# When the scan of one head pair may begin: waits taken per half instead of per pair, in a planned hybrid RWKV-7/GLA layer

## The chip, the cores and the metric

The kernel runs on one core of a Trainium2 chip. The metric is the device time of one execution in microseconds (us); lower is better. The engines that matter are TensorE (PE in the profile, PEld for its weight loads), VectorE (DVE), ScalarE (ACT), GpSimd (POOL) and SyncE (SP), which issues DMAs.

## The reference, cut to what matters

One layer over 256 latent tokens and 256 context tokens, width 2048, all in float32. A combined projection feeds an RWKV-7 branch (16 heads of 64 channels) and a GLA branch (4 heads); both scan in two directions, context first. The change lies in the RWKV-7 branch, whose recurrence for one head and one direction is

```
sa = S a_t
S  = S * w_t + sa b_t^T + v_t k_t^T
y  = S r_t
```

After it, the summed output `wkv` of both directions is normalized per head and token (mean and variance over 64 channels), gets a bonus term, is gated and goes through `w_a`; the GLA branch goes through `w_b`; the gated sum of both goes through `w_out`, the residual and a final RMSNorm.

## The kernel before, in words

Every float32 weight matrix is split into a high and a low part, and each product is three matmuls (`wH`, `wL` with the high and low part of the activations). This is the dense work; it comes as jobs of one 128-column slice each, in a list, and `stream` feeds them to TensorE. The RWKV-7 branch is done by eight head pairs `p`; a pair holds two heads in the 128 partitions.

The order of all instructions is made by a planner (`Issue`) when the program is built. Each piece of work is a generator (a track) that yields either an operation or list of operations, a claim on a PSUM bank, or a condition on a set `DONE`. `Issue.run` keeps an estimated clock for each engine and always emits the operation that can start earliest by these estimates; among PE operations within a small distance it takes the track with the lowest priority number, and the dense stream has 99, so that it fills what the others leave. The engines then run their queues in the emitted order, and hardware semaphores carry the real dependences. A condition on `DONE` is thus no instruction: it decides from which point in the emitted order on a track's operations may be placed. `Op` has the costs that the planner reckons with; for a two-input operation on POOL it is

```
149 + (1.667 if any(q == 0 and k > 1 for x in ins for q, k in x.ap[1:]) else 2.096) * n
```

nanoseconds for n elements per partition.

Tracks of a pair `p`: `fe_track` (features: decays, rates, keys; its second part asks for `gg`, `bt` and `bv` of pair p-1), `v_track` (loads values), `ab_track` and `inv_track` (a triangular inverse by 30 steps of two POOL operations each, `tm<-M` and `M<-M,tm`, a DVE transpose `Lin<-M`, PE products `pH` and `pZ`, and the evacuation into `Z`; it ends with `("gi", p)`), `gg_track` (chunk products into `GM` and `GMr`, six evacuations in three twos: context chunks, latent chunks 4 and 5, latent chunks 6 and 7), `bt_track` (transposed update rows into `BK`, for each direction `d` two groups `g` of four chunks), `mv_track` (transposed values into `UV`, two groups of four chunks; the group g asks that the scan of pair p-1 has passed step 4g+3), `aq_track` (copies by DMA), and `sc_track`, the scan.

`sc_track` makes eight steps: steps 0 to 3 over the context chunks and 4 to 7 over the latent ones, both directions at once. A step is a chain through four PE products and their evacuations: `p<-UV,GM`, `R<-p`, `pU<-R,Z`, `UV<-pU`, `pSs<-UV,BK`, `Sn<-pSs` and `UV<-Sn`. After step 7 it emits `("sc1", p)`, then waits for `("post", p-1)`, takes the mean of the output (`mu<-pY`, `xc<-pY,mu`), emits `("sc", p)`, and goes on with the normalization, the transpose `pyt`, the bias `yt` and the gate, and ends with `("post", p)`. `bv_track` of pair p+2 waits for `("post", p)`.

When the last pair's features and products are out, `"C"` is in `DONE`, and the jobs of the two branch projections may be taken once the jobs before them are done: first the 32 gate jobs (`tg`), then 16 slices of `w_b`, then 16 of `w_a`, whose activations are `yH` and `yL`, one slice per pair. The second half of each `w_a` slice asks for the normalized output of pair 7.

Of the kernel before, what the change touches and what calls it, by code (L numbers as in the profile page):

```python
# [76 lines left out]
class Issue:  # L77
# [136 lines left out]
    def rel(self, x):  # L214
        nm = x.tensor.name
        b = self.bank_of.pop(nm)
        self.busy.discard(b)
        self.bank_free[b] = self.rd.get(nm, 0.0)
# [112 lines left out]
def hybrid_layer(tc, a, out):  # L331
    nc = tc.nc
    es = ExitStack()
    with es:
# [331 lines left out]
        DONE = set()  # L666
# [423 lines left out]
        def past(p, i):  # L1090
            return lambda: p < 2 or ("st", p - 2, i) in DONE

        def bt_track(p, d, bk):

            BK = RW["BK"][p % 2]
            for g in range(2):
                yield past(p, 4 * g + 3)
                pt = yield Claim("g3", [P, 4, P], "pbt", bk)
                yield [PE.transpose(pt[:, n, :], bk[:, 4 * g + n].rearrange("p a b -> p (a b)"), ident) for n in range(4)]
                o = BK[:, :, 4 * g:4 * g + 4, d, :].rearrange("p h i c -> p i h c")  # L1100
                yield AC.copy(o if d == 0 else o[:, ::-1], pt.rearrange("p n (h c) -> p n h c", h=2))
                rel(pt)
            DONE.add(("bt", p) if ("bt", p, 1 - d) in DONE else ("bt", p, d))

        def ab_track(p, xp):

# [12 lines left out]
        def gg_track(p, fp, xp):  # L1119

            yield lambda: ("ab", p) in DONE
            s = RW[p]
            ar, bks = s["ar"], s["bks"]
            GM, GMr, BK = s["GM"], s["GMr"], s["BK"] = tuple(RW[n][p % 2] for n in ("GM", "GMr", "BK"))
            vs = rows(p)[1]
            xk = 1 - p % 2
            left = [6]

            def done():
                left[0] -= 1  # L1130
                if not left[0]:
                    DONE.add(("gg", p))

            def mask(m, n, r):
                return m[r, p % 2, None].to_broadcast([r.stop - r.start, n, 2, 64])

            def ev_c(pg, hd):
                yield DV.tensor_tensor(GM[vs, hd, 0:4], pg[vs], mask(m_ab, 4, vs), op=OP.mult)
                rel(pg)
                done()  # L1140

            def ev_l(pg, hd, i):
                yield DV.tensor_tensor(GM[vs, hd, 4 + i:6 + i], pg[vs, :, :, 0, :], mask(m_ab, 2, vs), op=OP.mult)
                yield DV.tensor_tensor(GMr[:, hd, i:i + 2], pg[:, :, :, 1, :], mask(m_r, 2, slice(0, P)), op=OP.mult)
                rel(pg)
                done()

            yield past(p, 3)
            pg = []
            for hd in range(2):  # L1150
                pg.append((yield Claim("g3", [P, 4, 2, 64], f"pgc{hd}", *bks, ar)))
            yield [PE.matmul(pg[hd][vs, i, d, :], bks[d][half(hd), chunk(i, d), xk, :], ar[half(hd), d, i, 0, :],
                             start=True, stop=True) for i in range(4) for d in range(2) for hd in range(2)]
            for hd in range(2):
                iss.spawn(3, ev_c(pg[hd], hd), "evc")
            iss.spawn(3, aq_track(p, xp), "aq")
            for i in (0, 2):
                yield past(p, 5 + i)
                pg = []
                for hd in range(2):  # L1160
                    pg.append((yield Claim("g3", [P, 2, 2, 2, 64], f"pgl{hd}", *bks, ar)))
                yield [PE.matmul(pg[hd][:, ii, d], bks[d][half(hd), chunk(4 + i + ii, d)].rearrange("p a b -> p (a b)"),
                                 ar[half(hd), d, i + ii, 1:3, :], start=True, stop=True)
                       for ii in range(2) for d in range(2) for hd in range(2)]
                for hd in range(2):
                    iss.spawn(3, ev_l(pg[hd], hd, i), "evl")
# [71 lines left out]
        def mv_track(p, fp, xp):  # L1238

            yield lambda: ("vc", p) in DONE  # L1240
            UV, vc = RW["UV"], RW["vc", p]
            vs = rows(p)[1]
            for g in range(2):
                yield lambda: p == 0 or ("st", p - 1, 4 * g + 3) in DONE
                pV = yield Claim("g3", [P, 2, 2, 64], "pV", vc)
                yield [PE.transpose(pV[:, x].rearrange("p h v -> p (h v)"), vc[:, 256 * g + P * x:256 * g + P * x + P], ident)
                       for x in range(2)]
                for par in range(2):
                    i0, i1 = 4 * g + par, 4 * g + 3 - par
                    yield AC.copy(UV[vs, i0:i0 + 3:2, 0], pV[half(par)])  # L1250
                    yield AC.copy(UV[vs, i1 - 2:i1 + 1:2, 1], pV[half(par), ::-1])
                rel(pV)
            DONE.add(("vdone", p))
            DONE.add(("mv", p))

        def sc_track(p, xp):

            yield lambda: all((x, p) in DONE for x in ("gi", "aq", "mv", "bt")) and (p == 0 or ("sc", p - 1) in DONE)
            s = RW[p]
            Dt, GM, GMr, BK, Z = (s[x] for x in ("Dt", "GM", "GMr", "BK", "Z"))  # L1260
            UV, rq = RW["UV"], RW["rq"]
# [1 line left out]
            DH = [(d, hd) for d in range(2) for hd in range(2)]  # L1263
            pY = Sc = None
            for i in range(8):
                if i == 4:
                    pY = yield Claim("py", [P, 4, 64], "pY")
                    yield PE.matmul(pY.rearrange("p c v -> p (c v)"), zb[:, 0:P], zb, start=True, stop=False,
                                    skip_group_check=True)
                p1 = yield Claim("st", [P, 2, 64], "p1", *(UV[:, i, :, hd, :] for hd in range(2)))  # L1270
                kr = slice(0, P) if i else vs
                b = [PE.matmul(p1[half(hd), d, :], GM[kr, hd, i, d, :], UV[kr, i, d, hd, :], start=True, stop=True)
                     for d, hd in DH]
                if i > 0:
                    SD = xp.tile([P, 2, 64], F32, name="SD", tag="SD", bufs=1)
                    b += [AC.activation(SD[:, d, :], Sc[:, d, :], AF.Copy, scale=Dt[:, i, d:d + 1]) for d in range(2)]
                yield b
                if i >= 4:
                    yield [PE.matmul(pY[half(hd), chunk(i, d) - 4, :], rq[us, d, i - 4, hd, :], UV[us, i, d, hd, :],
                                     start=False, stop=False, skip_group_check=True) for d, hd in DH]  # L1280
                R = xp.tile([P, 2, 64], F32, name="R", tag="R", bufs=1)
                yield AC.copy(R, p1)
                rel(p1)
                pU = [None, None]
                for hd in range(2):
                    pU[hd] = yield Claim(("st", "u1")[hd], [P, 2, 64], f"pU{hd}", R)
                yield [PE.matmul(pU[hd][half(hd), d, :], Z[half(hd), 2 * i + d, :], R[half(hd), d, :], start=True, stop=True)
                       for d, hd in DH]
                yield [(DV.tensor_copy if hd else AC.copy)(UV[us, i, :, hd, :], pU[hd][half(hd)]) for hd in range(2)]
                rel(pU[0])  # L1290
                rel(pU[1])
                pS = yield Claim("st", [P, 2, 64], "pSs", *(UV[:, i, :, hd, :] for hd in range(2)))
                yield [PE.matmul(pS[half(hd), d, :], BK[:, hd, i, d, :], UV[:, i, d, hd, :], start=True, stop=True)
                       for d, hd in DH]
                if i >= 4:
                    yield [PE.matmul(pY[half(hd), chunk(i, d) - 4, :], GMr[:, hd, i - 4, d, :], UV[:, i, d, hd, :],
                                     start=False, stop=i == 7, skip_group_check=True) for d, hd in DH]
                Sn = xp.tile([P, 2, 64], F32, name="Sn", tag="Sn", bufs=2)
                if i == 0:
                    yield [DV.tensor_scalar(Sn[:, d, :], pS[:, d, :], Dt[:, i, d:d + 1], None, op0=OP.mult) for d in range(2)]  # L1300
                else:
                    yield [DV.scalar_tensor_tensor(Sn[:, d, :], pS[:, d, :], Dt[:, i, d:d + 1], SD[:, d, :],
                                                   op0=OP.mult, op1=OP.add) for d in range(2)]
                rel(pS)
                Sc = Sn
                DONE.add(("st", p, i))
                if i < 7:
                    yield [(AC.copy if hd else DV.tensor_copy)(UV[us, i + 1, :, hd, :], Sn[half(hd)]) for hd in range(2)]
# [503 lines left out]
```

## Time and profile before

| | before |
|---|---|
| median of 3 runs | 1364.46 us (1361.43 to 1368.26) |
| the profiled execution's own time | 1361.36 us |
| its span, first to last instruction | 1359.6 us |
| mean granted TensorE clock | 0.977 of full speed |
| PE busy | 1270.1 us (93%) |
| DVE, ACT, POOL busy | 968.3, 718.2, 543.3 us |

The span is what the trace covers; the execution's own time holds 1.76 us more around it. Almost every instruction is recorded on line 304, since a helper emits them, so groups are told apart by the tiles they write and read (`UV<-pV` is written UV, read pV). The eight scans lie between about 690 and 1158 us.

### The profile page before, as it was taken

The numbers are of one execution on the slowest core, as the hardware profiler recorded it, in microseconds if no ns is written. First come the engines' busy times: TensorE is split into PE (matmuls) and PEld (weight loads), VectorE is DVE, ScalarE is ACT, GpSimd is POOL, SyncE is SP. The second block draws the span as 40 slices with busy tenths as digits, with TensorE's granted clock in tenths as the row PEclk, the third lists the DMA queues.
The fourth block names the chain that finished last, engine by engine and source line by source line (L and its number), as shares of the span: only waits on it lengthen the run. The fifth ranks groups of instructions, "written<-read, shape, count | busy, mean of one in ns | idle before, by whom it ended". The sixth has DMA issues, their size and how long they took to land. (4 is left out here: it accounts for less than half of the span.)

```text
span 1359.6 us, 29662 instructions
## 1 busy us (share of the span) xinstructions
PE 1270.1 (93%) x11479; PEld 1068.1 (79%) x11479; DVE 968.3 (71%) x2031; ACT 718.2 (53%) x1449; POOL 543.3 (40%) x684
## 2 busy tenths in 40 slices
PE   5999999999999999999899999799989999999996
PEld 3555578688788897998777778677878888999876
DVE  4433497885965737767978998698978776668656
ACT  5222244343334444486577678667766666445443
POOL 0000476676570000005888729673983550000012
PEclk9999999999999999999889999799979999999999
DMA  9999465455462433576632443234433545789564
GB/s 347 354 340 311 132 195 168 150 171 160 145 202 79 134 102 97 153 196 171 157 85 76 113 118 92 77 99 114 108 78 94 138 105 145 203 247 271 185 230 144
DMA packets 311186, 220.45 MB, mean 162 GB/s; under 512 B 37354, under 2 KB 286724, under 8 KB 310532
## 3 DMA queue, kind: packets, MB, share of 16 engines
q1 hardware_dynamic: 311044, 218.55, 55.5%
q8 instruction: 90, 1.47, 0.4%
q14 instruction: 52, 0.43, 0.1%
HBM read 199.76 MB, written 12.46 MB: 156 GB/s over the span
## 5 line engine op out<-in xcount | busy, mean ns | idle before, releaser
L304 DVE TENSOR_TENSOR wL<-raw,wH 128x512 fp32r<-128x512 f32 x484 | 377.2, 786 | 170.2 <-ACT wH L304 165.0
L304 ACT CAST wH<-raw 128x512 fp32r<-128x512 f32 x484 | 295.1, 616 | 328.5 <-PE acc L304 208.7
L304 PE MATMUL acc<-lH,wH 128*128 128x256 f32 x896 | 285.1, 318 | 0.5 <-ACT tg L304 0.5
L304 PE MATMUL acc<-lL,wH 128*128 128x256 f32 x896 | 256.0, 286 | 0.0
L304 PE MATMUL acc<-lH,wL 128*128 128x256 f32 x896 | 255.6, 285 | 0.2 <-DVE wL L304 0.2
L304 PEld LDWEIGHTS acc<-lH,wH 128*128 128x128 f32 x896 | 173.4, 194 | 21.1 <-issue 4.5
L304 POOL TENSOR_TENSOR tm<-M 64x30 f32<-64x30 f32 (+14 forms) x240 | 160.1, 667 | 74.3 <-DVE M L304 48.1
L304 POOL TENSOR_TENSOR M<-M,tm 64x30 f32<-64x30 f32 (+14 forms) x240 | 170.1, 709 | 18.7
L304 PEld LDWEIGHTS acc<-lL,wH 128*128 128x128 f32 x896 | 174.5, 195 | 3.1 <-issue 1.7
L304 PEld LDWEIGHTS acc<-lH,wL 128*128 128x128 f32 x896 | 173.9, 194 | 0.4 <-DVE wL L304 0.4
L304 PE MATMUL acc<-hH,wH 128*128 128x512 f32 (+1 forms) x416 | 168.7, 406 | 1.3 <-ACT lo L304 1.3
L304 PE MATMUL acc<-hH,wL 128*128 128x512 f32 (+1 forms) x416 | 157.2, 378 | 0.0
L304 PE MATMUL acc<-hL,wH 128*128 128x512 f32 (+1 forms) x416 | 156.3, 376 | 0.1
L304 PEld LDWEIGHTS acc<-hH,wH 128*128 128x128 f32 x416 | 78.6, 189 | 38.1 <-issue 22.9
L304 POOL TENSOR_TENSOR xs<-yg,fg 128x512 f32<-128x512 f32 (+1 forms) x10 | 13.5, 1371 | 231.4 <-DVE yg L304 231.4
L304 POOL TENSOR_TENSOR gw<-gw,csl 128x512 f32<-128x512 f32 x60 | 71.1, 1185 | 61.9 <-DMA gw<-in_w_mod_dram 61.9
L304 PEld LDWEIGHTS acc<-hH,wL 128*128 128x128 f32 x416 | 78.4, 188 | 15.5 <-DVE wL L304 0.4
L304 POOL TENSOR_TENSOR ga<-ga,gw 128x512 f32<-128x512 f32 x60 | 88.6, 1476 | 4.2
L304 PEld LDWEIGHTS acc<-hL,wH 128*128 128x128 f32 x416 | 78.9, 190 | 10.6 <-DVE hL L304 0.4
L304 PE MATMUL acc<-yH,wH 128*128 128x256 f32 x256 | 73.0, 285 | 0.0
L304 PE MATMUL acc<-yL,wH 128*128 128x256 f32 x256 | 72.8, 284 | 0.0
L304 PE MATMUL acc<-yH,wL 128*128 128x256 f32 x256 | 72.8, 284 | 0.0
(318 smaller groups left out, 2627.7 us busy)
## 6 DMA issues: line engine op xcount, KB each, us to landing
raw<-in_w_in_dram SPq DMA_DIRECT2D x174, 512.0 KB, 4.0
wm<-in_w_mod_dram SPq DMA_DIRECT2D x64, 512.0 KB, 6.9
gw<-in_w_mod_dram SPq DMA_DIRECT2D x64, 256.0 KB, 4.0
raw<-in_w_out_dram SPq DMA_DIRECT2D x32, 512.0 KB, 4.8
raw<-in_w_b_dram SPq DMA_DIRECT2D x16, 512.0 KB, 4.1
raw<-in_w_a_dram SPq DMA_DIRECT2D x16, 512.0 KB, 4.9
kv<-kvo SPq DMA_DIRECT2D x16, 256.0 KB, 3.9
tg<-tg SPq DMA_DIRECT2D x32, 128.0 KB, 3.8
```

The costliest lines, as they stand in the source:

```text
L304: op = Op("dma" if name == "dma_start" else self.key, name, lambda: f(*a, **k), aps[0], aps[1:], func, k.get("accum_out"), any(x.tensor.na ...
```

## The change

`sc_track` of pair p started when `gi`, `aq`, `mv` and `bt` of its pair were all complete and `("sc", p-1)` was there, that is, after the subtraction of the mean of pair p-1. It now starts at `gi`, `aq`, `("sc1", p-1)` (step 7 of pair p-1 emitted) and group 0 of the values, of both directions' update rows and of the chunk products. Group 1 of values and update rows and the next two evacuations of chunk products are asked for before step 4, the last two before step 6. No operation is added, removed or changed.

```
-            DONE.add(("bt", p) if ("bt", p, 1 - d) in DONE else ("bt", p, d))
+                DONE.add(("bt", p, d, g))
+            if ("bt", p, 1 - d, 1) in DONE:
+                DONE.add(("bt", p))
...
             def done():
                 left[0] -= 1
+                if left[0] % 2 == 0:
+                    DONE.add(("gg", p, 6 - left[0]))
                 if not left[0]:
                     DONE.add(("gg", p))
...
                 rel(pV)
+                DONE.add(("mv", p, g))
             DONE.add(("vdone", p))
-            DONE.add(("mv", p))
 
         def sc_track(p, xp):
 
-            yield lambda: all((x, p) in DONE for x in ("gi", "aq", "mv", "bt")) and (p == 0 or ("sc", p - 1) in DONE)
+            def there(g):
+                return lambda: all(x in DONE for x in (("mv", p, g), ("bt", p, 0, g), ("bt", p, 1, g), ("gg", p, 2 + 2 * g)))
+
+            yield lambda: ("gi", p) in DONE and ("aq", p) in DONE and (p == 0 or ("sc1", p - 1) in DONE)
+            yield there(0)
...
             for i in range(8):
+                if i == 6:
+                    yield lambda: ("gg", p, 6) in DONE
                 if i == 4:
+                    yield there(1)
```

## Rows read from the trace of the kernel before

**Rows 1.** The page's busy times: engine, busy us (share) x instructions.
```profile
PE 1270.1 (93%) x11479; PEld 1068.1 (79%) x11479; DVE 968.3 (71%) x2031; ACT 718.2 (53%) x1449; POOL 543.3 (40%) x684
```

**Rows 2.** Windows: stretch, length, busy per engine (instructions), granted clock, DMA share, GB/s.
```profile
690.00:1121.00 431.00, 397.42 (x5127) 338.62 (x5126) 359.83 (x782) 300.83 (x654) 292.91 (x430) 0.95 0.39 100
1121.00:1158.00 37.00, 36.86 (x435) 31.44 (x434) 21.54 (x57) 22.24 (x64) 0.00 (x0) 1.00 0.52 140
1158.00:1257.00 99.00, 99.00 (x835) 98.76 (x836) 73.38 (x154) 48.22 (x89) 0.00 (x0) 1.00 0.84 245
```

**Rows 3.** The chain that ended last: start, us, what.
```profile
1172.27 84.60 PE acc L304 x705
```

**Rows 4.** Tiles tg and yH: duration ns min/median/max, first and last start.
```profile
L304 ACT ACTIVATE tg<-acc x32: 362/380/397, 589.1 to 1164.4; 128x256 f32<-128x256 f32 x32
...
L304 PE MATMUL acc<-yH,wH x256: 279/283/387, 1163.7 to 1256.3; 128*128 128x256 f32 x128
...
L304 ACT CAST yH<-yt x1: 400/400/400, 1169.4 to 1169.4; 128x256 fp32r<-128x256 f32 x1
```

**Rows 5.** Timeline, scan of pair 0 to scan of pair 1: start, us, instruction.
```profile
747.71 0.48 DVE L304 SCALAR_TENSOR_TENSOR Sn<-pSs,Dt,SD 128x64 f32<-128x64 f32 x2
...
749.49 0.42 DVE L304 TENSOR_TENSOR xc<-pY,mu 128x256 f32<-128x256 f32 x1
...
750.82 0.36 ACT L304 COPY UV<-pV 64x256 f32<-64x256 f32 x1
...
751.41 0.31 PEld L304 LDWEIGHTS p<-UV,GM 64*64 64x64 f32 x8
```

**Rows 6.** Windows: last Sn of a pair to first R of the next, seven times.
```profile
748.20:751.90 3.70, 3.70 (x43) 3.24 (x41) 3.46 (x10) 2.65 (x7) 3.31 (x6) 1.00 0.87 193
797.40:801.10 3.70, 3.70 (x77) 3.37 (x76) 3.58 (x12) 3.53 (x9) 0.00 (x0) 1.00 0.83 212
860.20:882.00 21.80, 20.00 (x244) 17.26 (x242) 14.85 (x34) 19.14 (x29) 12.39 (x22) 0.79 0.27 70
936.40:951.10 14.70, 11.74 (x105) 9.94 (x102) 10.87 (x30) 12.57 (x21) 9.98 (x20) 0.88 0.34 87
1009.60:1012.50 2.90, 2.90 (x35) 2.44 (x34) 2.31 (x7) 1.92 (x6) 2.59 (x5) 1.00 0.14 17
1067.80:1071.80 4.00, 4.00 (x46) 3.54 (x43) 3.30 (x12) 3.65 (x10) 3.45 (x8) 1.00 0.92 198
1113.20:1121.20 8.00, 8.00 (x146) 7.39 (x142) 6.99 (x20) 6.88 (x14) 0.00 (x0) 1.00 0.38 101
```

**Rows 7.** Timeline, scan of pair 3 to scan of pair 4.
```profile
940.00 0.41 DVE L304 TENSOR_TENSOR xc<-pY,mu 128x256 f32<-128x256 f32 x1
...
941.33 1.12 PE L304 MATMUL pbt<-ident,bk 128*128 128x128 f32 x4 [2.96 <-ACT BK L304]
...
948.66 1.28 ACT L304 COPY UV<-pV 64x256 f32<-64x256 f32 x4
```

**Rows 8.** Timeline, the last evacuation into Z of pairs 3, 5 and 7.
```profile
874.98 0.69 DVE L304 COPY Z<-pZ 32x512 f32<-32x512 f32 x1
...
1008.36 0.69 DVE L304 COPY Z<-pZ 32x512 f32<-32x512 f32 x1 [0.58 <-ACT Z L304]
...
1120.30 0.69 DVE L304 COPY Z<-pZ 32x512 f32<-32x512 f32 x1 [0.20 <-ACT Z L304]
```

**Rows 9.** Timeline, the longest PE stall among the scans.
```profile
857.68 2.03 DVE L304 STREAM_TRANSPOSE Lin<-M 64x1024 f32<-64x1024 f32 x1 [5.61 <-POOL M L304]
...
859.76 1.06 PE L304 MATMUL pH<-Lin,GMo 32*32 32x32 f32 x32 [6.89 <-DVE Lin L304]
```

**Rows 10.** Window: the stretch of that stall and what followed it.
```profile
852.50:866.00 13.50, 6.61 (x98) 6.12 (x92) 6.98 (x13) 4.72 (x6) 6.34 (x16) 0.62 0.09 29
```

**Rows 11.** Timeline, one POOL operation of the inverse in two of the eight pairs.
```profile
842.72 2.66 POOL L304 TENSOR_TENSOR M<-M,tm 64x220 f32<-64x220 f32 x1
...
1094.31 1.11 POOL L304 TENSOR_TENSOR M<-M,tm 64x220 f32<-64x220 f32 x1
```

## The prediction, made before the changed kernel was run

> **What bounds the kernel now.** I read the page's busy times first: PE is busy 93% of the span, the next engine 71% [rows 1]. A share over the whole span says little here, so the windows come next: among the scans (690 to 1121 us) PE is busy 397 of 431 us, in the last scan nearly always, and from 1158 to 1257 us without a gap [rows 2]. The chain that ended last says the same of that stretch: one piece of 84.6 us made of dense matmuls alone [rows 3]. So the question is what a scan's end releases. Pair 7's normalized output becomes `yH` at 1169.4 us [rows 4]. Its readers are the second halves of the `w_a` slices. The branch matmuls on `yH` run from 1163.7 to 1256.3 us, and the 16 slices of `w_b` are the first half of them, so the `w_a` half begins near 1163.7 + 92.6/2 = 1210 us. The last scan is some 40 us early. What waits behind the scans is not their result but PE's own backlog: the last of the 32 gate jobs is evacuated at 1164.4 us [rows 4], after the last scan step, so there was dense work to be had during all eight scans.
>
> From this follows the rule by which I cost the change. PE has a fixed amount of work. If a scan begins earlier, the dense matmuls that filled its wait are done later, at the same price, in the stretch where PE never stops. The end moves only by PE time that was idle, or that ran at half clock.
>
> **The handovers.** The change acts between the last `Sn` of one pair and the first `R` of the next. I looked at the timeline of one of them: `Sn` of pair 0 is written by 748.19 us, the mean is subtracted by 749.91, the second group of pair 1's values is copied by 751.18, and the first products of scan 1 load their weights at 751.41 [rows 5]. The last to come was thus the value copy, not the normalization: the group may be transposed only after step 7 of the pair before, and the old condition wanted it for step 0. The windows of the seven handovers sum to 58.8 us [rows 6]. Two of them the change can't shorten: `Z` of pair 3 is complete at 875.67 and of pair 7 at 1120.99 us [rows 8], near the ends of these waits, and `("gi", p)` is still asked for. The other five are 3.7, 3.7, 14.7, 2.9 and 4.0, together 29.0 us.
>
> **What is removed.** From the old start to `R` the products and the copy take about 1 us (751.41 to the window's end at 751.9, and as much for the hand-over of `Sn`: an estimate). The five waits could shrink by 29.0 - 5 x 1.0 = 24.0 us, of which pair 4 has 13.7. For pair 5 this holds only while its scan stays behind `Z`, which is ready at 1009.05 us, 0.5 us before the handover [rows 6, 8]; once the scan of pair 4 ends 13.7 us earlier, scan 5 waits for its inverse instead. So the scan chain gains between 24 us, if the inverses move up with it, and 3.7 + 3.7 - 2.0 = 5.4 us up to pair 3, where `Z` was last in any case.
>
> What is that worth on PE? In the five waits PE is busy 3.70 + 3.70 + 11.74 + 2.90 + 4.00 = 26.04 of 29.0 us [rows 6]. The idle rest, 2.96 us, is one wait, of `pbt` for a copy on ACT [rows 7]. The granted clock in that window is 0.88 of full; at the half level (1.2 instead of 2.4 GHz) this is 0.12/0.5 = 24% of 14.7, 3.5 us, worth half of it, 1.7 us. Bounds: nothing, if the `pbt` wait stays where it is, and 2.96 + 1.7 = 4.7 us, if the earlier scan fills it. I take 4.7, since with scan 4 under way PE has something else in its queue just there.
>
> **What is moved.** The instructions are the same, DMAs included. The mean and its subtraction (0.41, 0.17 and 0.42 us in the handover) now lie beside the first step of the next scan on DVE, 1.0 us per pair, covered by the 40 us that the last scan is early; without that cover 7 us. PSUM bank of `pY`: it is claimed at step 4, over 20 us later, so nobody waits.
>
> **What is added.** New conditions: second group of values and update rows before step 4, products before steps 4 and 6. A scan takes about 50 us for eight steps (751.9 to 797.4 us, 882.0 to 936.4 [rows 6]), so step 4 is some 20 us after step 0, while the copies of the second value group end 3 us after the scan before in pair 1 and 14 in pair 4 [rows 5, 7]. I cost them at nothing; if the cover were gone, step 4 of one pair would wait up to the 14 us, again beside dense work.
>
> **The sum.** 1361.36 us (the profiled execution) - 4.7 = 1356.7. The median of the runs shown is 3.1 us above the profiled execution, so on that scale 1359.8; I say 1360. On this kernel about 0.5%, 6.8 us, is what a measurement can tell from no change.
>
> **Rivals.** The emitted order of everything after the first handover will differ, and the engines run their queues in that order. This gives a rival on each side.
>
> *B, faster: the stalls go.* Among the scans PE is idle 431 - 397.4 = 33.6 us, and a granted clock of 0.95 costs up to 0.05 x 431 = 21.6 us more [rows 2]. The largest piece is at 852.9: 6.89 us in which `pH` waits for a DVE transpose, which waits 5.61 us for POOL [rows 9], and then a stretch at clock 0.62 of 13.5 us, worth 0.38 x 13.5 = 5.1 us if PE were busy in it [rows 10]. If the new order puts this transpose further back, 6.9 + 5.1 = 12.0 us go besides the 4.7: 1361.4 - 16.7 + 3.1 = 1348. For it: a stage that is up to 24 us shorter has less time for stalls. Against it: the stall comes from POOL, which the change does not touch.
>
> *C, slower: the inverse comes too late for the new order.* The planner's cost for the POOL operation with 220 elements is 149 + 2.096 x 220 = 610 ns; it took 1.11 us in one pair and 2.66 in another [rows 11]. So the planner believes an inverse done earlier than it is, and puts the transpose and `pH` into the queues of DVE and PE where they may have to wait, with everything behind them. The old waits of 24 us gave POOL time to catch up, with dense work in them; a tighter order takes that time out and returns it as stalls that nothing fills. It decides where a transpose stands in DVE's queue ahead of POOL's last step. Price: one more stall as the one shown, 12.0 us, at pair 5, where the advance by then could be 19 us, and one of 5.4 us at pair 3: 1361.4 + 17.4 + 3.1 = 1382; with one alone 1370 to 1377. The Trainium skill speaks for this rival: SBUF — State Buffer, section "Who interferes with whom", says that a DVE instruction with both inputs in SBUF and a GpSimd instruction exclude each other on a shared port, so that the later one waits for the whole of the other. The trace agrees so far as the same POOL operation varies from 1.11 to 2.66 us [rows 11]; by this rule DVE work packed closer would make inverses longer still, and C would lie at its upper price; by the row alone either price could come.
>
> *D: the starts don't move,* since `gi` or the inverse's chain is last everywhere: 1361.4 + 3.1 = 1364.5. Against it: five handovers in which `Z` was ready before the values.
>
> The same skill's TensorE: Matmul & The Clock Gate, section "What's actually happening", says that the clock is low unless activity keeps it up. The trace agrees: the window around the idle 6.89 us has a granted clock of 0.62 [rows 10]. It makes each stall of B and C dearer than its idle time, which their prices already hold from the row.
>
> **How the numbers follow.** Forecast 0.44 (0.30 within 0.5%, 0.12 faster, 0.02 slower), B 0.28 (0.26 faster, 0.02 the same), C 0.23 (0.22 slower, 0.01 the same), D 0.05 (0.03 the same, 0.02 slower). Faster 0.38, the same 0.36, slower 0.26. The forecast's own range is 1354 to 1367: 1359.8 with the 4.7 us missed, or with half of B's 12.0 us added. The range for 8 in 10 reaches to B with a second stall of the 4.7 us kind gone (1348 - 4.7 = 1343) and to C (1382, with little beyond 1380): 1342 to 1380.
>
> **What would show it.** Right: the first `R` of pairs 1, 2, 4 and 6 within about 1 us of the last `Sn` before; the scans' end earlier by 5 to 24 us; more dense matmuls after it, at the same rate; PE's idle time among the scans smaller by 3 us and not much else. B: the 6.89 us wait of `pH` gone, the clock in the windows higher. C: more or longer waits of `Lin<-M` for POOL and of `pH` for DVE, and PE busy less of the stretch. The prediction is wrong if PE's idle time in the stage moves by more than 7 us either way, or if PE runs out of dense work.

## The result, and the profile after

The changed kernel took 1372.43 us (median of 8 runs, 1366.45 to 1377.9) against 1364.09 us for the kernel before (8 runs, 1359.0 to 1370.16). The ratio is 1.0061, 95% interval 1.0032 to 1.0090: slower by a little more than the half per cent that I had set as the bound. I had forecast 1360 us.

The page of the changed kernel begins with its busy times, as [rows 1]:

```profile
span 1372.0 us, 29669 instructions
...
PE 1273.9 (93%) x11479; PEld 1068.6 (78%) x11479; DVE 965.8 (70%) x2031; ACT 717.3 (52%) x1449; POOL 547.8 (40%) x684
```

The number of matmuls is the same. The span is 12.4 us longer; 3.8 us of that is time in which PE is busy and 8.6 us time in which it is idle. The medians differ by only 8.3 us: each profile shows one execution, the one before a fast one of its kernel, the one after a slower one of its own. So some 4 us of what this pair of profiles shows is scatter. To see where the time goes, I cut both executions at the first `R` and the last `Sn` of the eight scans. Windows of the kernel before, ahead of the scans, in them and behind them:

```profile
0.00:691.80 691.80, 648.63 (x4619) 524.22 (x4620) 452.90 (x942) 304.59 (x562) 238.42 (x248) 0.99 0.63 187
691.80:1158.60 466.80, 433.07 (x5555) 369.08 (x5555) 380.41 (x838) 321.41 (x716) 291.34 (x427) 0.96 0.40 103
1158.60:1359.60 201.00, 188.41 (x1309) 174.79 (x1308) 134.99 (x253) 92.17 (x173) 13.54 (x10) 0.99 0.70 214
```

and of the changed kernel:

```profile
0.00:694.40 694.40, 650.84 (x4620) 526.11 (x4621) 449.73 (x942) 304.56 (x561) 238.37 (x248) 0.99 0.63 186
694.40:1171.00 476.60, 435.14 (x5569) 369.10 (x5569) 382.61 (x840) 321.35 (x717) 295.94 (x427) 0.96 0.39 102
1171.00:1372.00 201.00, 187.88 (x1295) 173.34 (x1293) 133.47 (x251) 91.36 (x172) 13.50 (x10) 0.98 0.69 213
```

The 2.6 us ahead of the scans are scatter: up to there both programs are the same. Behind the scans both need 201.0 us. What is left, 9.8 us, lies among the scans: 476.6 instead of 466.8 us, with PE idle for 41.5 instead of 33.7 us.

The seven handovers, to be read against [rows 6]:

```profile
751.00:752.60 1.60, 1.60 (x20) 1.36 (x18) 1.60 (x5) 1.14 (x3) 1.50 (x2) 1.00 0.49 96
801.00:801.80 0.80, 0.80 (x12) 0.63 (x11) 0.80 (x2) 0.60 (x2) 0.00 (x0) 1.00 0.48 164
857.60:886.00 28.40, 21.86 (x262) 17.97 (x256) 20.20 (x42) 18.74 (x29) 24.82 (x49) 0.82 0.26 63
935.80:937.70 1.90, 1.47 (x16) 1.20 (x16) 1.82 (x5) 0.90 (x3) 0.00 (x0) 1.00 0.47 100
998.10:1011.70 13.60, 11.65 (x192) 10.48 (x191) 9.14 (x25) 10.28 (x14) 0.00 (x0) 0.85 0.22 59
1063.80:1077.00 13.20, 11.35 (x192) 10.18 (x191) 8.70 (x25) 9.42 (x13) 0.00 (x0) 0.87 0.54 102
1120.40:1133.60 13.20, 12.18 (x217) 11.43 (x216) 11.87 (x27) 8.62 (x17) 1.10 (x5) 1.00 0.57 152
```

The starts of pairs 1, 2 and 4 moved as the change wants: 2.1, 2.9 and 12.8 us less wait. Pairs 3, 5, 6 and 7 wait 6.6, 10.7, 9.2 and 5.2 us longer, 31.7 together against 17.8 gained. (The scans themselves became 4 us shorter together, so that the stretch is 9.8 us longer and not 13.9.) What they wait for is the inverse. The last evacuation into `Z` and the first `R` of pairs 3, 5, 6 and 7 in the timeline (the lines between are left out):

```profile
885.53 0.69 DVE L304 COPY Z<-pZ 32x512 f32<-32x512 f32 x1
885.93 0.26 ACT L304 COPY R<-p 128x128 f32<-128x128 f32 x1
...
1008.88 0.69 DVE L304 COPY Z<-pZ 32x512 f32<-32x512 f32 x1 [2.49 <-ACT Z L304]
...
1011.63 0.24 ACT L304 COPY R<-p 128x128 f32<-128x128 f32 x1
...
1074.43 0.69 DVE L304 COPY Z<-pZ 32x512 f32<-32x512 f32 x1 [2.47 <-ACT Z L304]
...
1076.95 0.27 ACT L304 COPY R<-p 128x128 f32<-128x128 f32 x1
...
1132.12 0.69 DVE L304 COPY Z<-pZ 32x512 f32<-32x512 f32 x1
...
1133.48 0.26 ACT L304 COPY R<-p 128x128 f32<-128x128 f32 x1
```

For pair 6 the trace shows why `Z` is late. The first POOL operation of its inverse, in the kernel before:

```profile
991.25 0.24 POOL L304 TENSOR_TENSOR tm<-M 64x30 f32<-64x30 f32 x1
```

and in the changed one:

```profile
1012.33 0.24 POOL L304 TENSOR_TENSOR tm<-M 64x30 f32<-64x30 f32 x1 [16.91 <-DVE M L304]
```

Before, POOL went from pair 5's inverse straight to pair 6's. Now it stands idle for 16.91 us, until the matrix `M` of pair 6 is there: the features `ar` of this pair start 10.5 us later than before (984.2 against 973.7 us), the masked products `AB` 17 us and the transpose `M<-Lin` 24 us.

And where does PE stand idle now? Its waits among the scans (line that waited and for what, us in total, times, longest), first of the kernel before, then of the changed one:

```profile
PE pH L304 <- DVE Lin L304: 7.8, 3, 6.9
PE p L304 <- DVE UV L304: 6.0, 13, 1.9
PE pSs L304 <- DVE UV L304: 3.9, 9, 1.0
PE pbt L304 <- ACT BK L304: 3.0, 1, 3.0
```

```profile
PE p L304 <- DVE UV L304: 11.3, 18, 2.0
PE pSs L304 <- DVE UV L304: 8.4, 9, 4.8
PE pH L304 <- DVE Lin L304: 5.1, 4, 2.9
PE pU L304 <- ACT R L304: 3.6, 3, 1.6
PE pV L304 <- ACT BK L304: 3.1, 2, 1.7
```

The wait of `pbt` that I wanted to recover is gone from the list, and so is the 6.9 us wait of `pH`. (A wait for another copy into `BK` stands there now, that of `pV`; 1.44 us of it come at 943.20, early in scan 4.) In their place stand waits of the scan's own products for `UV`: 19.7 us where there were 9.9. The longest of them is the stall of rival C, with another product as its victim:

```profile
993.18 2.00 DVE L304 STREAM_TRANSPOSE Lin<-M 64x1024 f32<-64x1024 f32 x1 [5.13 <-POOL M L304]
...
995.22 0.29 DVE L304 COPY UV<-pU 64x128 f32<-64x128 f32 x1
...
995.57 0.58 PE L304 MATMUL pSs<-UV,BK 128*64 128x64 f32 x5 [4.79 <-DVE UV L304]
```

Here the transpose for pair 5 stands in DVE's queue ahead of the copy that the last step of scan 4 needs. DVE waits 5.13 us for POOL, and PE 4.79 us for DVE.

### The profile page after: what moved, and what is told of

The parts are those of the page before. It is cut to its first block, busy times and chain, and to the rows that moved or that the text cites. A ratio compares the mean times of both kernels' runs of the same rounds, so it can differ in the third digit from the quotient of the medians.

```text
span 1372.0 us, 29669 instructions
## 1 busy us (share of the span) xinstructions
PE 1273.9 (93%) x11479; PEld 1068.6 (78%) x11479; DVE 965.8 (70%) x2031; ACT 717.3 (52%) x1449; POOL 547.8 (40%) x684
## 4 chain that ended last, share of the span: by engine, by line
PE 54%; DVE 17%; POOL 13%; ACT 6%; DMA 5%; issue 5%; SPq 0%; DVEq 0%; ACTq 0%; POOLq 0%
PE acc L304 33%; POOL M L304 6%; POOL tm L304 6%; PE pv L304 6%; DVE wL L304 5%; PE pg L304 3%; DMA raw<-in_w_out_dram 2%; ACT Lin L304 2%; DVE kvo L304 1%; PE pS L304 1%; ACT wH L304 1%; PE pout L304 1%; DVE Lin L304 1%; DVE UV L304 1%; PE pU L304 1%
## 5 line engine op out<-in xcount | busy, mean ns | idle before, releaser
L304 POOL TENSOR_TENSOR M<-M,tm 64x30 f32<-64x30 f32 (+14 forms) x240 | 173.4, 722 | 18.7
L304 POOL TENSOR_TENSOR xs<-yg,fg 128x512 f32<-128x512 f32 (+1 forms) x10 | 13.5, 1365 | 229.8 <-DVE yg L304 229.8
```

Source lines behind the costliest of these rows:

```text
L304: op = Op("dma" if name == "dma_start" else self.key, name, lambda: f(*a, **k), aps[0], aps[1:], func, k.get("accum_out"), any(x.tensor.na ...
```

## The experiments

After the result two theories were left. Theory 1: the change costs time of its own, since earlier scans push the preparation of the next pairs back, or since inverses come too late for the tighter order. Theory 2: the change only draws another order from the planner, and the order before was a good draw.

**Which part of the change acts.** With `sc1` in the place of `sc` as the only edit, the planner emits the same order as before on every engine, line by line: alone, the tie to the other pair's normalization never decided a start. It was not run, being the same program. The other part without that one:

```
-            yield lambda: ("gi", p) in DONE and ("aq", p) in DONE and (p == 0 or ("sc1", p - 1) in DONE)
+            yield lambda: ("gi", p) in DONE and ("aq", p) in DONE and (p == 0 or ("sc", p - 1) in DONE)
```

> Parts asked for as the scan comes to them, but the start still tied to the previous pair's mean (sc instead of sc1). Theory 1 (the preparation of the next pairs, feature to inverse, is the loop that sets the scans, and the earlier scans push it back): like the changed kernel, 1368 to 1376 us, since the ask by halves is what moves the scans. Rival, theory 2 (the new order is merely another draw among orders that differ by some 10 us): anywhere from 1355 to 1378 us. Rival 3 (the mean, taken beside the next scan's first step, is the cost): back to 1364 us.

Measured: 1373.16 us, ratio 1.0065 (1.0042 to 1.0087). Rival 3 falls, and asking by halves is enough for the whole loss. Beside it the tie to the mean does decide something: the handovers to pairs 1 and 2 are 3.5 and 2.4 us in this trace, 1.6 and 0.8 in that of the changed kernel. The time does not show it.

**Which pair.** The old conditions for some pairs, the new ones for the others. The edit for new conditions in pair 4 alone; the other run has `p == 4` in its place:

```
+            if p != 4:
+                yield lambda: all((x, p) in DONE for x in ("gi", "aq", "bt")) and ("mv", p, 1) in DONE and (p == 0 or ("sc", p - 1) in DONE)
```

> New conditions for pair 4 alone, the pair with the 14.7 us handover. Theory 1: the scan of pair 4 starts some 13 us earlier, scan 5 waits for its inverse, the inverses of pairs 6 and 7 come later than before, and the time is 1368 to 1374 us. Theory 2: any time between 1355 and 1378 us, with the inverses of 6 and 7 on either side. My forecast's account (dense work is moved, the end stays): 1358 to 1364 us.

> New conditions for all pairs except pair 4. Theory 1: the other four handovers are 2 to 3 us each, so little is pushed back: 1362 to 1368 us. Theory 2: any time between 1355 and 1378 us.

Measured: 1367.39 us, ratio 1.0020 (0.9998 to 1.0042), with pair 4 alone; 1373.83 us, 1.0060 (1.0038 to 1.0082), with all but pair 4. The first is not told apart from the kernel before; it lies 0.6 us under theory 1's range and 3.4 us above the one of my forecast's account. The second is far from the 1362 to 1368 us of theory 1, which had it the other way round: new conditions in the pair with the large handover cost little, those in the other seven the whole.

**Mere reshuffles.** Among the operations of one engine, whichever it is, that can start within `win` nanoseconds of the earliest, the planner prefers the one with the higher priority. I moved that constant, in the old and in the new kernel, to 35 (shown), 30, 38, 42 and 45:

```
-                win = 40
+                win = 35
```

> The kernel before with a constant of the planner that has no meaning of its own shifted: the distance within which it prefers the higher priority, 35 instead of 40 ns. It shows how far a mere reshuffle moves the time. Theory 1: within 4 us of before, 1360 to 1368 us. Theory 2: as far as the change, some 8 us or more to either side.

> The kernel before with the planner's distance for preferring priority at 45 instead of 40 ns: a second mere reshuffle. After the run with 35 ns (ratio 1.0062) theory 2, that the old order is one of the better draws and any reshuffle costs about as much as the change, expects 1366 to 1378 us. Theory 1, that earlier scans push the preparation back, has no part here and expects before's time, 1360 to 1368 us, with the 35 ns run an exception.

> The changed kernel with 35 instead of 40 ns. Theory 1 (the change itself costs some 8 us on any order): some 8 us above the kernel before with 35 ns, so about 1380 us. Theory 2 (two draws from the same heap): 1360 to 1378 us, on either side of the kernel before with 35 ns.

> The changed kernel with 45 instead of 40 ns. Theory 1: some 8 us above the kernel before with 45 ns. Theory 2: 1360 to 1378 us, on either side of it.

> The kernel before with 30 instead of 40 ns, a third mere reshuffle. Theory 2: 1362 to 1378 us. Theory 1: 1360 to 1368 us.

> The changed kernel with 30 ns. If the change has a cost of its own: some 6 us above the old conditions at 30 ns, about 1388 us. If orders are draws: 1362 to 1385 us, more likely below those 1382 us than above, as that was the slowest draw so far.

> The kernel before with 38 ns. Draws: 1366 to 1382 us, above the kernel before, as the three others. If 40 ns was no special draw: 1360 to 1368 us.

> The changed kernel with 38 ns. Cost of its own: some 6 us above the old conditions at 38 ns. Draws: 1362 to 1382 us, on either side.

> The kernel before with 42 ns. Draws: 1366 to 1382 us. If 40 ns was no special draw: 1360 to 1368 us.

> The changed kernel with 42 ns, against 1375 us of the old conditions at 42 ns. A cost of its own: about 1383 us. Draws: 1362 to 1382 us, with a mean over the six pairs within 0.3% of nothing.

Measured, as ratios to the kernel before (95% intervals):

| win, ns | old conditions | new conditions | new less old, % |
|---|---|---|---|
| 30 | 1.0123 (1.0103 to 1.0142) | 1.0028 (1.0005 to 1.0051) | -0.95 |
| 35 | 1.0062 (1.0043 to 1.0081) | 1.0047 (1.0027 to 1.0067) | -0.15 |
| 38 | 1.0076 (1.0053 to 1.0099) | 1.0008 (0.9981 to 1.0036) | -0.68 |
| 40 | 1 (the kernel before) | 1.0061 (1.0032 to 1.0090) | +0.61 |
| 42 | 1.0057 (1.0034 to 1.0080) | 1.0079 (1.0051 to 1.0107) | +0.22 |
| 45 | 1.0081 (1.0054 to 1.0108) | 1.0116 (1.0097 to 1.0136) | +0.35 |

All five reshuffles of the old kernel are slower than it, by 0.57 to 1.23%: about as much as the change (0.61%), or more. The new conditions are faster in three pairs and slower in three. That is against theory 1, by which the last column would be near +0.5% in every line. The mean of the last column is -0.10%; its scatter is 0.61, so that the mean of six is known to about 0.64 (2.57 x 0.61 / square root of 6). This interval is on the narrow side: it takes the six for independent draws, while neighbouring constants give similar orders (35 and 38 ns leave 85% of the old kernel's PE instructions in the same place). Theory 2 holds in the main: the measured 0.61% lies within what another order costs (0.1 to 1.2% in these ten), and the change alone has no effect that these runs can tell from nothing. Neither a cost of its own of half a per cent nor the gain of 0.35% (4.7 us) that I forecast is excluded. Two draws fell outside the ranges given for theory 2, both above 1378 us: 1382.30 us (old, 30 ns) and 1380.95 us (new, 45 ns), the latter near what theory 1 expected there.

The late inverse of pair 6 is no work of the change either. Its `Z` is complete at 1058.0 us in the kernel before and at 1075.1 in the changed one, but at 1077 to 1084 us in the traces of all five reshuffles of the old kernel.

The slowest draw, the old conditions at 30 ns, shows the same kinds of waits as the changed kernel, though nothing of the change is in it (PE's waits among its scans):

```profile
PE p L304 <- DVE UV L304: 13.8, 15, 5.6
PE pH L304 <- DVE Lin L304: 5.8, 3, 3.4
PE pSs L304 <- DVE UV L304: 4.6, 11, 1.0
```

**Is the inverse the pace, or PE?** Every second step of the inverse left out, in both kernels:

```
-            for j in range(1, 31):
+            for j in range(1, 31, 2):
```

> The kernel before with every second of the 30 steps of the inverse left out (output not the reference's), so that POOL has about 22 us less per pair and Z comes earlier. If the inverses set the pace of the scans, the stretch from the first R to the last Sn becomes 30 us or more shorter than 467 us. If the end is set by PE's work, as I forecast, the dense work goes behind the scans and the time falls only by stalls: 1350 to 1370 us, the spread of orders included. If the scans set the end, it falls by 30 us or more, below 1335 us.

> The changed kernel with every second of the 30 steps of the inverse left out (output not the reference's). If the new start conditions gained nothing only because Z was last, their gain shows now: the scans take 15 to 24 us less than in the kernel before with half an inverse. If the end hangs on PE's work, the time is still within 10 us of that kernel's.

Measured: 1345.55 us, ratio 0.9849 (0.9817 to 0.9881), with the old conditions and 1349.95 us, 0.9878 (0.9832 to 0.9923), with the new. The windows of the scans, old and new:

```profile
664.80:1138.40 473.60, 443.36 (x5772) 379.87 (x5773) 368.87 (x874) 339.69 (x742) 148.92 (x235) 0.97 0.42 111
```

```profile
667.30:1134.30 467.00, 438.47 (x5670) 374.02 (x5671) 366.39 (x866) 335.23 (x731) 154.55 (x235) 0.96 0.41 107
```

POOL has half the work in this stretch and the first scan starts 27 us earlier, yet the eight scans still take 474 and 467 us (466.8 with the whole inverse). So POOL's part of the inverse does not give the scans their length. `Z` still comes last: in the old kernel it is complete within 2 us of the first `R` in six of the seven handovers. What delays it now lies ahead of the inverses, where POOL waits for `M` for 67.2 us in all, against 48.1 with the whole inverse. PE is busy 94% of the stretch, with 217 matmuls more in that window than before; that PE's work is what holds the preparation and the scans is my reading of this share, and no run isolates it. The time fell by some 20 us, to 4.5 us below the range I had given, and not below 1335 us, as it would if the scans set the end. The new conditions save 6.6 us of scans here, not 15 to 24, and their time is 4.4 us above that of the old ones. Of the old kernel's 18.0 us of span, 8.7 are idle PE (89.5 to 80.8) and 9.3 PE busy (1270.1 to 1260.8).

**Rival C by its cause.** The planner's cost of the inverse's POOL operations brought near what they take:

```
+        def dear(op):
+            op.cost *= 1.65
+            return op
...
+                yield dear(PO.tensor_tensor(M[:, j + 1:32, 0:j], M[:, j + 1:32, 0:j], tv, op=OP.add))
```

(and the multiplication before it likewise)

> The kernel before with the planner's cost of the 60 POOL operations of an inverse times 1.65, near what they take. My rival C (the planner believes the inverse done too early and queues transposes and products in front of other work) expects fewer waits for POOL and PE's idle time among the scans down by 5 to 10 us, 1352 to 1362 us. Theory 2 (any new order is a draw) expects 1360 to 1382 us like the other reshuffles.

> The changed kernel with the same cost. Rival C expects the change's loss to go, 1352 to 1364 us; theory 2 expects 1360 to 1382 us.

Measured: 1404.65 us, 1.0286 (1.0245 to 1.0327), old; 1402.42 us, 1.0267 (1.0225 to 1.0309), new. Both theories missed. The remedy cured what it was for: waits of `Lin` for POOL, 9.0 us in the kernel before, are gone from the list of waits. The time rose all the same. The window of the scans, old conditions:

```profile
718.00:1247.60 529.60, 475.40 (x5828) 412.77 (x5828) 390.54 (x862) 331.57 (x731) 242.00 (x412) 0.91 0.41 109
```

The scans are stretched to 529.6 us, PE is idle for 54.2 us in them, and its granted clock falls to 0.91. The waits of POOL in the same window tell where the stretch comes from:

```profile
POOL wh L304 <- DMA wl<-in_a_a_dram: 95.7, 3, 35.3
POOL wh L304 <- PE pbt L304: 34.9, 1, 34.9
...
POOL wh L304 <- PE pab L304: 18.5, 1, 18.5
```

`wh` is a copy of weights with which the features of a later pair begin; it is no part of the inverse. With the dearer inverse the planner puts that copy between two steps of it, and POOL's queue stands still until the copy can run. (In the kernel before it stands inside two of the inverses, without a wait.) In each of the first six pairs one such wait of 15 to 35 us lies inside the inverse, which takes 62 to 77 us from its first POOL operation to its last, against 42.5 to 51.5 us in the kernel before. So the run took away rival C's stalls but made the inverse itself longer, and it does not decide what C's stalls cost.

## Why the prediction was wrong, point by point

**What sets the end: right.** The stretch behind the scans is 201.0 us in both kernels. Pair 7's output is written into `yH` at 1181.4 us (1169.4 before, [rows 4]), while the branch matmuls on `yH` run from 1174.3 to 1268.1 us, so the `w_a` half begins near 1221, still 40 us later. The last gate job is evacuated at 1174.9 us: dense work was there throughout. The draws say the same: with the new conditions at 45 ns the last `Sn` comes at 1158.5 us, as in the kernel before (1158.6), and the stretch behind it takes 217.6 us instead of 201.0. The half inverses add that POOL's work in the inverse does not give the scans their length. The limit of the rule shows with the planner's dearer inverses: there the last gate job was done at 1075.1 us, 172 us before the scans ended, and in between PE was busy for 143.6 of 172.6 us.

**The handovers: right in place and size where they could move.** I gave pairs 1, 2 and 4 gains of 2.7, 2.7 and 13.7 us; they gained 2.1, 2.9 and 12.8. That scan 5 would then wait for its inverse was also right. That pair 6 would gain 3 us was wrong: its `Z` came 17 us later than before. For pair 3 I read 875.67 us as near the end of the wait; it lies 6.3 us before that end, so `Z` was not the last to come there; with the change it is.

**What it is worth on PE: the step that failed.** "I take 4.7, since with scan 4 under way PE has something else in its queue just there." The 3 us wait of `pbt` did go, though 1.44 us came back close by as a wait of `pV`. The failed step is the sum: it subtracts 4.7 us and has no other term. It thus left every other stall of the planned order in its place and put what a new order does to them at nothing, without a reason, although rivals B and C had just been built on it. Among the scans PE's idle time did not fall by 3 us; it rose by 7.8, from 33.7 to 41.5. In the traces of the thirteen other orders (the partial changes and the reshuffles) it is 36.7 to 46.6 us. I had named this condition myself ("wrong if PE's idle time in the stage moves by more than 7 us"), and yet gave a chance of 0.44 to outcomes in which the stalls stay. The reshuffles tell what that term should have been: with the same work, another order costs 0.1 to 1.2%, and on average of the ten reshuffles, five old and five new, +0.7%. The order before was better than all ten by their medians (the least of them, 0.08%, is not clear of noise), so the sum should have been made from the mean of such orders, not from the profile of a good one. Whether the 4.7 us themselves are there stays open: they are 0.35%, inside the interval of the six pairs.

**Two smaller errors of the working.** Rivals B and C price a stall at 6.9 + 5.1 us. The 5.1 count the low clock over the whole 13.5 us of [rows 10], the idle 6.89 us included, which are thus paid twice. From the end of the stall to 866 us PE was busy for 6.24 us at a granted clock of 0.51, which is worth 3.1 us. And the upper end of the forecast's own range, 1367, does not follow from the 4.7 us missed, which gives 1364.5. Neither made the forecast fail.

**Rival B: half of it happened.** The 6.89 us wait of `pH` [rows 9] went with the old order, as B said. As much came back elsewhere.

**Rival C: seen, but not a law.** Its stall at pair 5 is there: 5.13 us of DVE waiting for POOL, 4.79 us of PE behind it. But the waits of `Lin` for POOL rose only from 9.0 to 12.4 us. The cure of the planner's cost put other stalls on POOL and so does not settle the price of C. On the rule of the Trainium skill in SBUF — State Buffer, section "Who interferes with whom", on which C leaned: POOL's busy time among the scans went from 291.34 to 295.94 us for the same 427 instructions, 1.6% more (ahead of the scans, where the programs are the same, 238.42 and 238.37). So far the trace agrees in direction; that DVE caused it is not shown, and 4.6 us over eight pairs are too little to make the result.

**Rival D: wrong for pairs 1, 2 and 4,** right for half of the diff: the tie to the normalization, taken away by itself, changed no instruction's place. Once the halves are asked for, the tie does hold the starts of pairs 1 and 2, by some 2 us.

**What stays open:** why 40 ns with the old conditions is so good a draw. That its constants were chosen by measuring would explain it, but no run here shows that. An inverse of pair 6 that follows pair 5's at once is part of that order; it is not enough to make a good one, as the new conditions at 30 ns have it too and took 0.28% longer.

## What to carry to other kernels

Where a planner makes the order, a loosened condition does two things: it moves the waits it names, and it draws a new order for everything behind. Cost the second by reshuffles of the kernel before (a constant without meaning moved up and down a few times) before you read anything into the first: here the reshuffles spread over 1.2%, and the change stayed inside. Don't judge an order by the waits between its scans: with the new conditions at 30 and at 45 ns the seven handovers are 51.3 and 51.7 us together, less than the 58.8 before, and the time was 0.3 and 1.2% longer. By the accounting used here a wait that is full of dense work is worth nothing when it goes; only idle PE time and half clock are. And a profile of a good draw shows less idle PE time than the next order will.

## What the runs showed that I had not expected

Bringing the planner's cost of one engine's operations nearer to the truth (the inverse's at 1.65 times their cost) took all waits for that engine off the list and made the kernel 2.9% slower, more than any reshuffle: the planner put another track's copy into six of the inverses, and POOL waited there for up to 35 us. And five executions of one and the same stretch of program, up to the first scan, ended between 691.8 and 697.6 us (the kernels before and after and the three partial changes): a profile of one execution can't carry differences of that size.
